# Start offsets of the narrow weight tiles in SBUF: one offset for both parts, or 64 pairs of eight line offsets

## The chip, the cores and the metric

The kernel runs on one core of a Trainium2 chip. The metric is the device time of one execution in microseconds. The kernel before takes 3164.23 us, the median of 3 runs (3163.09 to 3170.76).

## What is computed

Two transformer-like blocks stand one behind the other, on 256 tokens (and, in the first block, 256 context tokens) of width 1024, all in fp32. The first block has two layers: half an FFN, a mixer, half an FFN; the mixer of layer 0 is a Fourier transform, that of layer 1 a bidirectional retention. The second block has two layers of FFN, mixer (HGRN2 scan and dilated window attention) and FFN. From the reference, cut:

```python
def swiglu(h, w_gate, w_up, w_down):
    return (jax.nn.silu(h @ w_gate) * (h @ w_up)) @ w_down

def half_ffn(t, m, j):
    h = modulate(rmsnorm(t, norm_g[l, j]), m[3 * j], m[3 * j + 1])
    return t + 0.5 * m[3 * j + 2] * swiglu(h, ...)

def retention_layer(h_lat, h_ctx, w_in, w_out, decay, cos, sin, need_ctx_out):
    qc, kc, vc, gc = ret_project(h_ctx, w_in)
    ...
    ql, kl, vl, gl = ret_project(h_lat, w_in)
    ...
    y_lat = ret_output(yl, gl, w_out)

for l in range(DEPTH):                                   # the second block
    x = x + 0.5 * swiglu_2(rmsnorm_2(x, ffn1_norm[l]), ffn1_w_in[l], ffn1_w_out[l])
    h = rmsnorm_2(x, mix_norm[l])
    hq, hf, hi, hg, aq, ak, av, ga, gb = jnp.split(h @ w_in[l], split_idx, axis=-1)
    ...
    x = x + merged @ w_out[l]
    x = x + 0.5 * swiglu_2(rmsnorm_2(x, ffn2_norm[l]), ffn2_w_in[l], ffn2_w_out[l])
```

Nearly all arithmetic is in the products of activations with weights, which are most of the 506 MB that the kernel reads from HBM.

## The kernel before

**Three matmuls for a product.** Every fp32 operand is split into an upper part, rounded to the format float32r, and a lower part, the rest. A product is three float32r matmuls, `mm3` (L270): upper by upper (L272), upper by lower (L273) and lower by upper (L274), summed in PSUM. A matmul has a stationary operand of 128 x 128, which a weight load (PEld) brings into the array, and a moving operand of 256, 258 or 512 columns. Each of the three has a weight load of its own.

**Weights.** `get` (L205) and `getw` (L222) hand out weight tiles in an order that a first, empty pass over the program has recorded (`plan`). `_dma` (L151) loads 1 MiB into a tile `raw`; `_split` (L159) makes the upper part `wh` from it on ScalarE (ACT, L166) and the lower part `wl` on VectorE (DVE, L167). There are three buffers each of `wh` and `wl`. Each has 2048 + 128 elements of 4 bytes per partition, 8704 bytes, and begins at a multiple of 512 bytes. The data begin `at` bytes into the buffer, for `wh` and `wl` alike: 0 for WIDE tiles, whose moving operand has 512 columns, 64 for NARROW ones, with 256 columns, 192 for MOVING ones. L164 and L165:

```python
wh = self.wsp.tile([128, 2048 + PAD // 4], F32R, name="wh", tag="wh")[:, at // 4:]
wl = self.wsp.tile([128, 2048 + PAD // 4], F32R, name="wl", tag="wl")[:, at // 4:]
```

**The two uses of a tile.** `gemm_t` (L566) has the weights stationary and the activations moving: three matmuls for each of 8 slices k of 128 rows, then the same for the next 128 output columns. In the trace their names read `mm<-s,wh` and `mm<-s,wl`. `gemm_n` (L594) has the activations stationary and 256 columns of weights moving (`mm<-wh,s`, `mm<-wl,s`). Activations lie in tiles `s`, slots of 2048 bytes that begin at multiples of 512 bytes. So in `gemm_t` the moving operand begins at a multiple of 512, and the stationary one `at` bytes behind one; in `gemm_n` it is the other way round. Products of two activations (`mm<-s,s`) have both at multiples of 512.

**The order of the work.** It is written out by hand: `body` (L1728) calls the layers one after the other, and `tick` puts a piece of other work (norms, the scan, attention) between two groups of matmuls. From `M.retention` (L1787) on the stream has 256 columns, apart from eight 512-column matmul groups of the keys in the retention layer (WIDE), and apart from the FFN behind the retention layer (`M.ffn(..., shift=True)`, L1795): there the tokens carry two more columns, 258 in all, and the tiles' offsets come from the table SHIFTED, 22 numbers from 12 to 208, most of them no multiple of 64. Retention's values and the mixers' `unit_n` (L1249) use `gemm_n`.

Of the kernel before, what the change touches and what calls it, by code (L numbers as in the profile page):

```python
# [10 lines left out]
F32R = mybir.dt.float32r  # L11
# [8 lines left out]
KT = 8  # L20
# [9 lines left out]
SCRATCH = 1024  # L30
GAP = 2048 - SCRATCH - 128

WIDE, NARROW, MOVING, PAD = 0, 64, 192, 512
SHIFTED = (12, 68, 72, 76, 80, 84, 52, 44, 204, 200, 208, 196, 140, 136, 132, 144, 40, 36, 100, 88, 160, 176)

VEC = [("c", 8), ("c_ctx", 8), ("ada_b", 144), ("norm_g", 48), ("final_g", 8), ("four_b", 8),
       ("ffn1_norm_2", 16), ("mix_norm_2", 16), ("ffn2_norm_2", 16), ("hgrn_lb_logits_2", 16),
# [53 lines left out]
class Ker:  # L91
    def __init__(self, tc, I, out, plan):
        self.tc, self.nc, self.I, self.out = tc, tc.nc, I, out
        self.V, self.A, self.T = self.nc.vector, self.nc.scalar, self.nc.tensor
        self.free = deque(range(NSLOT))
        self.where = {}
        self.plan = plan
        self.asked = []
        self.nraw = NRAW
        self.ndma = self.nspl = self.nget = 0  # L100
        self.wget, self.wsplit, self.hold = -1, 0, None
        self.rawt, self.splt = {}, {}
        self.bg = deque()
        self.urgent = deque()
        self.pend = deque()
        self.subs = deque()
        self.late = {}
        self.chains = []
        self.turn = 0
        self.uid = 0  # L110
        self.quiet = False
        self.lazy = False
        self.splim = None

    def pools(self, ctx):
# [43 lines left out]
    def _split(self, i):  # L159
        src, raw, at = self.plan[i]  # L160
        if raw:
            return
        t, v, n = self.rawt.pop(i)
        wh = self.wsp.tile([128, 2048 + PAD // 4], F32R, name="wh", tag="wh")[:, at // 4:]  # L164
        wl = self.wsp.tile([128, 2048 + PAD // 4], F32R, name="wl", tag="wl")[:, at // 4:]  # L165
        self.A.activation(wh[:, :n], t[:, :n], AF.Copy)  # L166
        self.subs.append((i, lambda: self.V.tensor_sub(wl[:, :n], t[:, :n], wh[:, :n].bitcast(F32))))  # L167
        k = src.shape[1]
        self.splt[i] = (wh[:, :n].rearrange("p (k c) -> p k c", k=k),
                        wl[:, :n].rearrange("p (k c) -> p k c", k=k))  # L170
# [48 lines left out]
            return self.rawt.pop(i)[1]  # L219
        return self.splt.pop(i)  # L220

    def getw(self, w, k0, k1, c0, c1, at=NARROW):  # L222
        return self.get(w.rearrange("(k p) m -> p k m", p=128)[:, k0:k1, c0:c1], at=at)


# [133 lines left out]
class Model(Ker):  # L359
# [345 lines left out]
    def ffn(self, X, wg, wu, wd, resid, after=None, shift=False):  # L705
        n = N2 + 2 if shift else N2
        cx, c = slice(0, n), slice(0, N2)
        for hi, (f0, f1) in enumerate(self.HALVES):
            G = Split(self, f1 - f0, N2)
            for f in range(f0, f1, 2):  # L710
                at = (SHIFTED[f], SHIFTED[f + 1]) if shift else (NARROW, NARROW)
                ug = self.getw(wg, 0, KT, 128 * f, 128 * f + 256, at[0])
                pg = [self.mm([128, n]) for _ in range(2)]
                for m in self.pair_t(pg, ug, X, cx, f == 0):
                    self.tick()
                uu = self.getw(wu, 0, KT, 128 * f, 128 * f + 256, at[1])
                pu = [self.mm([128, n]) for _ in range(2)]
                for m in range(2):
                    self.gemm_t(pu[m], uu, X, m, cx, 0, KT, True, True)
                    if f:  # L720
                        self.ffn_act(G, f - f0 + m, pg[m], pu[m], N2, self.rb, shift)
                    self.tick()
                if f == 0:
                    self.drain_urgent()
                    for m in range(2):
                        self.ffn_act(G, m, pg[m], pu[m], N2, self.rb, shift)
            if hi == 1:
                X.rel()
            self.flush()
            km = (f0 + f1) // 2  # L730
            for mp in range(4):
                pd = [self.mm([128, N2]) for _ in range(2)]
                if hi == 1 and mp == 3:
                    self.splim = self.nget + 3
                for k0, k1 in ((f0, km), (km, f1)):
                    u = self.getw(wd, k0, k1, 256 * mp, 256 * mp + 256)
                    for m in range(2):
                        self.gemm_t(pd[m], u, G, m, c, k0, k1, k0 == f0, k1 == f1, f0)
                        if k1 == f1:
                            resid(2 * mp + m, pd[m])  # L740
                            if after and hi == 1:
                                after(2 * mp + m)
                            self.tick()
            self.resume()
            G.rel()
# [502 lines left out]

    def unit_n(self, X, n, off):  # L1249
        c = self.COLS[n] + off  # L1250
        u = self.getw(self.w_in, 0, KT, c, c + 256, MOVING)
        ps = self.mm([128, 2, 256])
        for tt in range(2):
            self.gemm_n(ps[:, tt], u, X, tt)
            self.tick()
        return ps
# [471 lines left out]
def body(M, stop):  # L1728
    I, out = M.I, M.out
    upto = STOPS.index(stop or "all")  # L1730

    def dump():
        M.nc.sync.dma_start(out.rearrange("(k p) t -> p k t", p=128), M.x[:, :, :out.shape[1]])

    def w(l, j):
        return I["ffn_w_gate"][l, j], I["ffn_w_up"][l, j], I["ffn_w_down"][l, j]

    M.consts()
    first, r, xr = [], [], []

    def sums(s):
        for d in range(KT):
            M.stat(d, STREAM[s])

    H = Split(M, KT, N1)
    M.splim = LATE - 1
    sums(0)

    def latent():
        xr.append(M.lead(0, r[0]))  # L1750
        sums(1)
    M.ada_first(0, {2: lambda: r.append(M.rstd(LAT)), 4: latent})
    M.ada_first(1, {0: lambda: r.append(M.rstd(CTX)), 4: lambda: xr.append(M.lead(1, r[1]))})
    M.splim = LATE
    M.lazy = True
    first.append(M.getw(I["ffn_w_gate"][0, 0], 0, KT, 0, 256))
    M.lazy = False
    M.rel(M.sc32)
    M.lead_end(xr[0], 0, H, 0, KT)
    M.splim = LATE + 1  # L1760
    M.catch_up()
    M.urgent.extend([lambda d=d: M.lead_end(xr[1], 1, H, d, d + 4) for d in range(0, KT, 4)])
    M.bg.append(M.ada_silu)
    half = [lambda d, s, j=j: M.cm[:, 8 * j + d, s:s + 1] for j in range(2)]
    for ch in range(2, 8):
        M.bg.extend(M.ada_steps(0, ch))
    H = M.ffn2s(H, *w(0, 0), half[0], 1, M.dft_load, (5, 8, 1), first[0])
    if upto == 0:
        return dump()
    H = M.fourier(H, 2)  # L1770
    if upto == 1:
        return dump()
    for l, ch in ((0, 8), (1, 0), (1, 1), (1, 2), (1, 3)):
        M.bg.extend(M.ada_steps(l, ch))
    H = M.ffn2s(H, *w(0, 1), half[1], 0)
    if upto == 2:
        return dump()
    for ch in range(4, 9):
        M.bg.extend(M.ada_steps(1, ch))
    H = M.ffn2s(H, *w(1, 0), half[0], 1, M.ret_prep, (2, 1, 4))  # L1780
    while M.bg:
        M.tick()
    M.rel(*M.cb[0], *M.cb[1])
    if upto == 3:
        return dump()

    M.retention(H, lambda: M.shifted_begin(2), M.pre)  # L1787
    X = M.pre_end()
    if upto == 4:
        return dump()  # L1790
    M.final_begin()

    def resid(d, ps):
        M.resid(d, ps, half[1], LAT)
    M.ffn(X, *w(1, 1), resid, M.final_pre, shift=True)  # L1795
    if upto == 5:
        return dump()
    X = M.final_end()
    if upto == 6:
        M.drain_urgent()  # L1800
        M.tick()
        return dump()
    ov = out.rearrange("(k p) t -> p k t", p=128)
    for l in range(2):
        M.pre_begin("mix_norm_2", l)

        def ww(j):
            wi = I[f"ffn{j}_w_in_2"][l]
            return wi[:, :FF], wi[:, FF:], I[f"ffn{j}_w_out_2"][l]
        M.ffn(X, *ww(1), M.resid_half, M.pre)  # L1810
        if upto == 7 + 2 * l:
            return dump()
        X = M.mixer(l, M.pre_end())
        if upto == 8 + 2 * l:
            return dump()
        if l == 0:
            M.pre_begin("ffn1_norm_2", 1)
            M.ffn(X, *ww(2), M.resid_half, M.pre)
            X = M.pre_end()
        else:  # L1820
            M.ffn(X, *ww(2), M.resid_half, lambda d: M.nc.sync.dma_start(ov[:, d], M.x[:, d, :N2]))
# [28 lines left out]
```

## Time and profile before

| | |
|---|---|
| median of 3 runs | 3164.23 us (3163.09 to 3170.76) |
| the profiled execution | 3162.56 us |
| its span, first to last instruction | 3160.8 us |
| granted TensorE clock, mean | 0.996 of 2.4 GHz |
| TensorE busy (PE) | 3121.8 us, 99% |
| weight loads (PEld) | 2928.3 us, 93% |
| VectorE (DVE) | 2192.4 us, 69% |
| ScalarE (ACT) | 1368.3 us, 43% |
| DMA | 510.69 MB, 162 GB/s |

Matmuls are pipelined: a record lasts some 280 ns, but the next one begins 113 to 120 ns after it. What a matmul costs is the step from one start to the next. It is read from a stretch without idle time as its length over the number of matmuls in it, less 2.4 that had begun before the stretch (280 ns over a step). The retention layer begins at 1214.9 us of the span, the FFN with 258 columns at 1508.4, the second block at 1712.

### The profile page before, as it was taken

What the parts mean: (1) busy time and instruction counts of PE and PEld (TensorE: products, weight loads), DVE (VectorE), ACT (ScalarE), POOL (GpSimd) and SP (SyncE); (2) the same over time, 40 slices, a digit from 0 to 9 for tenths busy, and PEclk for the clock granted to TensorE, in tenths of its full rate; (3) what the DMA queues carried; (4) which work ended last, traced back from release to release, by engine and by line L of the source; (5) the groups of instructions that cost most, each with busy time, mean ns of one, the idle gap of its engine ahead of it and who ended that gap; (6) DMA issues with size and microseconds to landing.
All of it is one profiled execution on the core that took longest, in us unless ns stands there. A gap on an engine that the chain in (4) does not pass through costs nothing.

```text
span 3160.8 us, 53819 instructions
## 1 busy us (share of the span) xinstructions
PE 3121.8 (99%) x22520; PEld 2928.3 (93%) x22520; DVE 2192.4 (69%) x4077; ACT 1368.3 (43%) x1945; POOL 0.5 (0%) x5
## 2 busy tenths in 40 slices
PE   7999999999999999999999999999999999999999
PEld 5888898888888889999999999999999999999999
DVE  6797578874666537566767678867756668877755
ACT  3223353222422225443545456654545446655543
POOL 0000000000000000000000000000000000000000
PEclk9999999999999999999999999999999999999999
DMA  7465414563246533233555654444555655444563
GB/s 285 166 224 178 136 54 134 182 204 123 91 156 216 185 107 108 94 123 119 170 189 188 201 188 152 160 147 134 186 190 185 198 184 171 152 156 134 177 198 121
DMA packets 431699, 510.69 MB, mean 162 GB/s; under 512 B 8800, under 2 KB 396128, under 8 KB 431456
## 3 DMA queue, kind: packets, MB, share of 16 engines
q1 hardware_dynamic: 428736, 503.35, 48.0%
q10 hardware_dynamic: 2720, 3.90, 0.4%
q8 instruction: 177, 2.90, 0.4%
q14 instruction: 66, 0.54, 0.0%
HBM read 506.16 MB, written 1.05 MB: 160 GB/s over the span
## 4 chain that ended last, share of the span: by engine, by line
PE 92%; DVE 5%; ACT 1%; issue 1%; DMA 1%; SPq 0%; ACTq 0%; DVEq 0%
PE mm L272 29%; PE mm L274 29%; PE mm L273 29%; PE mm L1465 2%; DVE wl L167 1%; ACT wh L166 1%; DVE x L672 1%; PE mm L1624 1%; DVE s L523 0%; DMA raw<-in_ada_n 0%; PE aux L1674 0%; PE mm L1608 0%; DVE s L520 0%; DVE sqs L483 0%; PE mm L580 0%
## 5 line engine op out<-in xcount | busy, mean ns | idle before, releaser
L272 PE MATMUL mm<-s,wh 128*128 128x256 f32 (+2 forms) x5872 | 1813.5, 309 | 3.5 <-ACT s L521 2.5
L273 PE MATMUL mm<-s,wh 128*128 128x256 f32 (+2 forms) x5872 | 1804.7, 307 | 2.9 <-DVE s L523 0.8
L274 PE MATMUL mm<-s,wl 128*128 128x256 f32 (+2 forms) x5872 | 1803.3, 307 | 3.2 <-DVE wl L167 3.1
L273 PEld LDWEIGHTS mm<-s,wh 128*128 128x128 f32 x5872 | 1112.6, 189 | 63.0 <-DVE s L523 4.1
L274 PEld LDWEIGHTS mm<-s,wl 128*128 128x128 f32 x5872 | 1108.6, 189 | 61.5 <-DVE wl L167 4.8
L272 PEld LDWEIGHTS mm<-s,wh 128*128 128x128 f32 x5872 | 1107.6, 189 | 62.4 <-ACT s L521 3.7
L167 DVE TENSOR_TENSOR wl<-raw,wh 128x2048 fp32r<-128x2048 f32 (+2 forms) x438 | 928.9, 2123 | 239.2 <-ACT wh L166 239.1
L166 ACT ACTIVATE wh<-raw 128x2048 fp32r<-128x2048 f32 (+2 forms) x438 | 777.1, 1779 | 594.6 <-PE mm L273 221.3
L457 DVE SCALAR_TENSOR_TENSOR jk<-raw,s 128x512 bf16<-128x512 f32 x448 | 309.2, 690 | 12.2
L272 PE MATMUL mm<-wh,s 128*128 128x256 f32 x960 | 273.6, 285 | 0.0
L767 ACT ACTIVATE s<-tmp 128x256 fp32r<-128x256 f32 (+1 forms) x176 | 87.8, 499 | 418.4 <-DVE tmp L753 320.3
L273 PE MATMUL mm<-wl,s 128*128 128x256 f32 x960 | 267.4, 279 | 0.0
L274 PE MATMUL mm<-wh,s 128*128 128x256 f32 x960 | 267.3, 278 | 0.0
L753 DVE TENSOR_TENSOR tmp<-tmp,mm 128x512 f32<-128x512 f32 x66 | 45.3, 686 | 196.7 <-PE mm L274 161.2
L273 PEld LDWEIGHTS mm<-wl,s 128*128 128x128 f32 x960 | 180.9, 188 | 0.2
L272 PEld LDWEIGHTS mm<-wh,s 128*128 128x128 f32 x960 | 180.8, 188 | 0.3
L274 PEld LDWEIGHTS mm<-wh,s 128*128 128x128 f32 x960 | 180.5, 188 | 0.0
L672 DVE SCALAR_TENSOR_TENSOR x<-mm,cm,x 128x256 f32<-128x256 f32 x160 | 71.8, 479 | 106.6 <-PE mm L274 106.5
L769 DVE TENSOR_TENSOR s<-tmp,s 128x256 fp32r<-128x256 f32 (+1 forms) x176 | 91.3, 519 | 2.2 <-ACT s L767 0.5
L765 DVE TENSOR_TENSOR tmp<-mm,sqs 128x256 f32<-128x256 f32 x88 | 36.8, 419 | 67.9 <-PE mm L274 67.7
L764 ACT ACTIVATE tmp<-tmp 128x256 f32<-128x256 f32 x88 | 36.2, 412 | 103.8 <-DVE tmp L763 103.7
L772 DVE SCALAR_TENSOR_TENSOR x<-mm,x 128x256 f32<-128x256 f32 x64 | 27.0, 423 | 53.9 <-PE mm L274 53.7
(247 smaller groups left out, 2028.5 us busy)
## 6 DMA issues: line engine op xcount, KB each, us to landing
raw<-in_ffn_w_in SPq DMA_DIRECT2D x88, 1024.0 KB, 4.9
raw<-in_w_in SPq DMA_DIRECT2D x84, 1024.0 KB, 4.8
raw<-in_ada_t SPq DMA_DIRECT2D x64, 1024.0 KB, 5.2
raw<-in_ffn_w_gate SPq DMA_DIRECT2D x44, 1024.0 KB, 5.1
raw<-in_ffn_w_up SPq DMA_DIRECT2D x44, 1024.0 KB, 5.1
raw<-in_ret_w_in SPq DMA_DIRECT2D x24, 1024.0 KB, 4.9
raw<-in_ffn_w_out SPq DMA_DIRECT2D x32, 768.0 KB, 4.6
raw<-in_ffn_w_down SPq DMA_DIRECT2D x32, 640.0 KB, 4.0
```

The lines of the kernel that those rows point to most:

```text
L166: self.A.activation(wh[:, :n], t[:, :n], AF.Copy)
L167: self.subs.append((i, lambda: self.V.tensor_sub(wl[:, :n], t[:, :n], wh[:, :n].bitcast(F32))))
L272: T.matmul(ps, ah, bh, start=first, stop=False)
L273: T.matmul(ps, ah, bl, start=False, stop=False)
L274: T.matmul(ps, al, bh, start=False, stop=last)
L457: V.scalar_tensor_tensor(jk, r[:, j, 512 * i:512 * i + 512], 1.0, self.cb[s][i], OP.mult, OP.mult, accum_out=a[:, 2 * q + j, s, i:i + 1])
L672: self.V.scalar_tensor_tensor(self.x[:, d, e], ps[:, e.start - c.start:e.stop - c.start], gate(d, s), self.x[:, d, e], OP.mult, OP.add)
L753: V.tensor_mul(g, sg, pu)
L765: V.tensor_mul(g, pu, rb)
L767: A.activation(G.h(f), g, AF.Copy)
L769: self.defer(lambda: V.tensor_sub(G.l(f), g, G.h(f).bitcast(F32)))
L1465: T.matmul(ps[:m, a, b], kc, qc, start=True, stop=True)
```

## The change

`getw` without an offset numbers the tiles. Up to the retention layer both parts still begin at 64. From there on (`M.later = True`) tile number 8i + j has its upper part at 64 j bytes and its lower part at 64 ((3j + i) mod 8) bytes; over 64 tiles these are all 64 pairs of 0, 64, ..., 448. The table SHIFTED and the offset MOVING go: the FFN with 258 columns and `unit_n` take pairs too. WIDE tiles stay at 0. The instructions of every engine are the same ones in the same order; start addresses alone differ, in 12,930 matmuls, in their weight loads, and in the ACT and DVE instructions that write `wh` and `wl`.

```diff
-WIDE, NARROW, MOVING, PAD = 0, 64, 192, 512
-SHIFTED = (12, 68, 72, 76, 80, 84, 52, 44, 204, 200, 208, 196, 140, 136, 132, 144, 40, 36, 100, 88, 160, 176)
+WIDE, NARROW, PAD = (0, 0), (64, 64), 512
...
+        self.later, self.narrow = False, 0
...
-        wh = self.wsp.tile([128, 2048 + PAD // 4], F32R, name="wh", tag="wh")[:, at // 4:]
-        wl = self.wsp.tile([128, 2048 + PAD // 4], F32R, name="wl", tag="wl")[:, at // 4:]
+        wh = self.wsp.tile([128, 2048 + PAD // 4], F32R, name="wh", tag="wh")[:, at[0] // 4:]
+        wl = self.wsp.tile([128, 2048 + PAD // 4], F32R, name="wl", tag="wl")[:, at[1] // 4:]
...
-    def getw(self, w, k0, k1, c0, c1, at=NARROW):
+    def getw(self, w, k0, k1, c0, c1, at=None):
+        if at is None:
+            i, j = divmod(self.narrow, 8)
+            at = (64 * j, 64 * ((3 * j + i) % 8)) if self.later else NARROW
+            self.narrow += 1
         return self.get(w.rearrange("(k p) m -> p k m", p=128)[:, k0:k1, c0:c1], at=at)
...
             for f in range(f0, f1, 2):
-                at = (SHIFTED[f], SHIFTED[f + 1]) if shift else (NARROW, NARROW)
-                ug = self.getw(wg, 0, KT, 128 * f, 128 * f + 256, at[0])
+                ug = self.getw(wg, 0, KT, 128 * f, 128 * f + 256)
...
-        u = self.getw(self.w_in, 0, KT, c, c + 256, MOVING)
+        u = self.getw(self.w_in, 0, KT, c, c + 256)
...
+    M.later = True
     M.retention(H, lambda: M.shifted_begin(2), M.pre)
```

## Rows read from the trace of the kernel before

**Rows 1.** The page: span, and part 1, busy time of each engine.
```profile
span 3160.8 us, 53819 instructions
...
PE 3121.8 (99%) x22520; PEld 2928.3 (93%) x22520; DVE 2192.4 (69%) x4077; ACT 1368.3 (43%) x1945; POOL 0.5 (0%) x5
```

**Rows 2.** The page, part 4: the chain that ended last, by engine.
```profile
PE 92%; DVE 5%; ACT 1%; issue 1%; DMA 1%; SPq 0%; ACTq 0%; DVEq 0%
```

**Rows 3.** Who waited for whom, PE alone: total us, times, longest us.
```profile
PE mm L274 <- DVE wl L167: 3.1, 5, 0.9
```

**Rows 4.** Windows, PE alone: start:end, length, busy us (matmuls in it), clock, DMA share, GB/s.
```profile
1275.00:1280.00 5.00, 5.00 (x44) 1.00 0.41 143
1508.40:1579.30 70.90, 70.03 (x584) 1.00 0.51 162
1613.30:1671.00 57.70, 57.70 (x483) 1.00 0.49 152
1717.00:1887.00 170.00, 170.00 (x1503) 1.00 0.61 196
...
2440.00:2612.00 172.00, 172.00 (x1520) 1.00 0.59 192
2990.00:3157.00 167.00, 167.00 (x1420) 1.00 0.50 163
```

**Rows 5.** Timeline of PE from 400.37, every third instruction: start us, length us, instruction.
```profile
400.37 0.28 PE L272 MATMUL mm<-s,wh 128*128 128x256 f32 x1
...
400.71 0.28 PE L272 MATMUL mm<-s,s 128*128 128x256 f32 x1
...
401.07 0.28 PE L272 MATMUL mm<-s,s 128*128 128x256 f32 x1
...
401.43 0.28 PE L272 MATMUL mm<-s,s 128*128 128x256 f32 x1
```

**Rows 6.** Timeline of PE from 2071.67, every third instruction.
```profile
2071.67 0.28 PE L272 MATMUL mm<-wh,s 128*128 128x256 f32 x1
...
2072.01 0.28 PE L272 MATMUL mm<-wh,s 128*128 128x256 f32 x1
...
2072.35 0.28 PE L272 MATMUL mm<-s,wh 128*128 128x256 f32 x1
...
2072.70 0.28 PE L272 MATMUL mm<-s,wh 128*128 128x256 f32 x1
...
2073.05 0.28 PE L272 MATMUL mm<-s,wh 128*128 128x256 f32 x1
```

**Rows 7.** Timeline of PE from 1899.78, every third instruction.
```profile
1899.78 0.28 PE L272 MATMUL mm<-s,wh 128*128 128x256 f32 x1
...
1900.13 0.29 PE L272 MATMUL mm<-wh,s 128*128 128x256 f32 x1
...
1900.49 0.28 PE L272 MATMUL mm<-wh,s 128*128 128x256 f32 x1
...
1900.83 0.28 PE L272 MATMUL mm<-wh,s 128*128 128x256 f32 x1
```

**Rows 8.** Groups of PE by form from 1214.9 on: count, busy us, mean ns, idle before.
```profile
L273 PE MATMUL mm<-s,wh 128*128 128x256 f32 x3569 | 997.1, 279 | 1.9 <-DVE s L1352 0.7 <-DVE s L1108 0.3 <-DVE s L523 0.3
L273 PE MATMUL mm<-wl,s 128*128 128x256 f32 x960 | 267.4, 279 | 0.0
L273 PE MATMUL mm<-s,wh 128*128 128x258 f32 x352 | 99.5, 283 | 0.0
```

**Rows 9.** The same of 1717:1887, then of 2990:3157.
```profile
L273 PE MATMUL mm<-s,wh 128*128 128x256 f32 x501 | 138.3, 276 | 0.0
...
L273 PE MATMUL mm<-s,wh 128*128 128x256 f32 x474 | 133.2, 281 | 0.0
```

**Rows 10.** Groups of DVE, the lower part's split: of 1613.3:1671, then of 2990:3157.
```profile
L167 DVE TENSOR_TENSOR wl<-raw,wh 128x2048 fp32r<-128x2048 f32 (+1 forms) x11 | 23.6, 2143 | 8.1 <-ACT wh L166 8.1
...
L167 DVE TENSOR_TENSOR wl<-raw,wh 128x2048 fp32r<-128x2048 f32 (+2 forms) x34 | 67.1, 1975 | 27.5 <-ACT wh L166 27.5
```

More of the change, by code (lines that the diff above doesn't have):

```diff
@@ L715, in ffn @@
                     self.tick()
-                uu = self.getw(wu, 0, KT, 128 * f, 128 * f + 256, at[1])
+                uu = self.getw(wu, 0, KT, 128 * f, 128 * f + 256)
                 pu = [self.mm([128, n]) for _ in range(2)]
```

## The prediction

> **What bounds the kernel now.** I read the page's busy times first: PE 99%, weight loads 93%, VectorE 69%, ScalarE 43% [rows 1]. The chain that ended last is PE for 92% [rows 2], and of PE's waits for a part of a weight tile there are five, 3.1 us in all [rows 3]. So the time is the number of matmuls times the step from one to the next. The edit takes away no matmul and moves none. It can act only on the step, or on the splits that write the tiles.
>
> Then I read the step, stretch by stretch, from the windows. It isn't one number, though shape and granted clock (1.00, the 2.4 GHz level) are the same [rows 4]:
> - **short**, 113.3 ns: the first FFN of the second block, 1717 to 1887 us. 170 us / (1503 - 2.4). Its twin in the next layer has 172 / (1520 - 2.4) = 113.3.
> - **middle**, 117.8 ns: the last FFN, 2990 to 3157. 167 / (1420 - 2.4).
> - **long**, 120.2 ns: products of two activations in the retention layer, 1275 to 1280. 5.00 / (44 - 2.4). The FFN with 258 columns has 70.03 / (584 - 2.4) = 120.4 in its first half and 57.7 / (483 - 2.4) = 120.1 in its second.
>
> Short and middle occur for the same tiles at the same offset, 64 bytes for both parts, hundreds of matmuls on end. So the offset alone doesn't fix the step; how the stream came into the stretch does too. What an offset does at a border without a wait, three timelines tell; three steps are 0.34 us if short, 0.35 if middle, 0.36 if long.
> - Up to 400.71 the stream is short, with weights at 64 and activations at 0. Then products of two activations begin, both at 0, and every three steps take 0.36 [rows 5]. The short step is lost at once.
> - Up to 2072.35 it is short with the moving weights at 192 and the stationary activations at 0; with stationary weights at 64 it is middle, 0.35 [rows 6]. Lost again.
> - At 1900.13 the reverse: from stationary weights at 64 to moving ones at 192, 0.35, then 0.36, then 0.34 [rows 7]. Here a change of offset wins the short step.
>
> So: the short step stays only while nothing changes, and another offset may set the stream into another step.
>
> **The change, part by part.** From 1214.9 us on, line L273 has 3569 matmuls with stationary and 960 with moving weights of 256 columns; times three lines, 10,707 and 2,880, together 13,587. With 258 columns there are 352 x 3 = 1,056 [rows 8]. How many are short now I take from the mean length of a record, which follows the step: 276 ns in the short stretch, 281 in the middle one [rows 9]. Both forms have 279 over the whole part [rows 8]. (281 - 279) / (281 - 276) = 40% short, 5,435; 60% middle, 8,152.
>
> 1. *Offsets differ from tile to tile.* A tile lasts 30 to 48 matmuls, and now each one brings another pair, where two FFNs ran through some 1,500 matmuls with one offset. Two of the three borders above lose the short step, and the one that wins it lies between the other two uses of a tile. I take it that the 5,435 become middle: 5,435 x (117.8 - 113.3) = +24.5 us. Bounds: all 8,152 middle ones become short, -36.7 us; or everything becomes long, 5,435 x 6.9 + 8,152 x 2.4 = +57.1 us. I choose the middle step because it is nearest to most rows: it is what the same operands fall into when they don't keep the short one.
> 2. *Both parts differ within a tile.* The three matmuls of a slice load upper, upper and lower part, so in 56 of 64 pairs the offset changes twice in three matmuls. No row shows that. If each change only costs what the border at 1900.13 cost, 0.02 us, the price is unbounded by the trace short of the long step in 1. I count nothing beside it.
> 3. *Line 0 is among the eight.* Offset 0 against activations at 0 is the pair of operands that has the long step. 8 of 64 pairs have their upper part there (two of three loads), 8 their lower part (one of three): (16 + 8) / 192 = 1/8 of the loads. 13,587 / 8 x (120.2 - 117.8) = +4.1 us. Bounds 0 and, if 256 acts as 0 does, +8.2. That it may is read from 64 against 0 and 0 against 192: differences of 64 and -192, equal but for 256, and both know the short step.
> 4. *Some short steps remain or are won*, as at 1900.13. An eighth of term 1: -3.1 us. Bounds are those of 1.
> 5. *The FFN with 258 columns* gives up a table of its own. It runs at 120.1 to 120.4 now, which is the long step already. Nothing, between -6.2 (1,056 x 5.9, all as short as the short step with two columns more, 114.2) and +1.
> 6. *The splits.* Where the table's offsets apply, the lower part takes 2143 ns, else 1975 [rows 10]: 0.17 us less for each of 22 tiles. It lies beside the matmuls, whose waits for it are 3.1 us in all, so nothing; a slower PE gives it more room still. Were that cover gone, it would be worth 3.7 us.
>
> Sum: 24.5 + 4.1 - 3.1 = **+25.5 us** on 3162.6, the profiled execution's own time (span 3160.8): 3188. The median of the runs shown is 1.7 above that execution, so I predict 3189 us.
>
> A rule speaks against all of it. The Trainium skill, "SBUF — State Buffer", section "Who interferes with whom", gives PE two independent read ports, one for the moving operand and one for weight loads, and says that "PE and ACT never wait on anyone". By that rule a start address would be worth nothing, and the time would stay at 3164. The trace disagrees here: with nothing but the start address of the stationary operand changed, the step goes from 113.3 to 120 ns at 400.71.
>
> **The rivals.**
> - *Long steps spread.* If multiples of 256 act as 0 does, 28 of 64 pairs hold at least one, and a tile may run long as a whole: 24.5 + 0.44 x 13,587 x 2.4 = +39 us, 3203. For it: the long step is what the 258 columns have at nearly all of their 22 offsets. Against: it is seen with 256 columns only where both operands begin at 0.
> - *Faster: the short step catches the stream.* A long run of the middle step can't leave it now, because nothing disturbs it; the FFN of 2990 to 3157 stays there to the end. Ever new offsets throw it out, as at 1900.13, and if the short step holds over all those pairs, the stream stays in it. With three quarters of the middle steps: -27.5 us, 3137. The point from which this decides is a share of short steps over today's 40%. Against: two of three borders lost the short step, and one of them by going to offset 0, which the pairs hold.
> - *Nothing happens*, or losses and gains balance: 3164, within 0.3%, or 9.5 us, which is about what a measurement of this kernel tells from no change. For it: stretches of both kinds exist now, and a new mix may come out at 40% again.
> - That the change doesn't do what it says I leave at under one in a hundred: the flag is set in the pass that records the plan and in the one that uses it.
>
> **How the numbers follow.** The forecast, 3180 to 3198, has 0.48; long steps spread 0.22; the short step catches 0.16; nothing 0.14. Faster by over 0.3% 0.16, within it 0.14, slower 0.70. The range goes from 3150, which leaves out most of the faster case, to 3214, nearly the bound with everything long (3221).
>
> **What would show it.** In the profile after, the stretch of the second block's first FFN holds some 1,440 matmuls in 170 us instead of 1,503; the mean record of L273 with 256 columns goes from 279 to 281 ns; the mean of the 258 columns stays at 283. Waits of PE for `wl` stay at some 3 us. I am wrong if the FFN at 1717 keeps 113 ns, or if the last FFN falls from 117.8 to it; and wrong in size if windows there show 120 or more.

## The result: 3185.0 us, and the profile after

| | before | after |
|---|---|---|
| median of 3 runs, us | 3164.23 (3163.09 to 3170.76) | 3185.04 (3184.93 to 3185.19) |
| profiled execution, us | 3162.6 | 3185.0 |
| its span, us | 3160.8 | 3183.2 |

The ratio is 1.006, with an interval of 1.0037 to 1.0083: slower. The forecast was 3189, its case 3180 to 3198.

The page of the changed kernel: the span, the busy time of each engine, and the chain that ended last by engine.

```profile
span 3183.2 us, 53819 instructions
...
PE 3144.2 (99%) x22520; PEld 2950.9 (93%) x22520; DVE 2193.2 (69%) x4077; ACT 1367.7 (43%) x1945; POOL 0.5 (0%) x5
...
PE 93%; DVE 5%; ACT 1%; issue 1%; DMA 1%; SPq 0%; ACTq 0%; DVEq 0%
```

Against [rows 1, 2], the counts of instructions are the same on every engine, VectorE and ScalarE are as busy as they were, and PE's busy time alone has grown by 22.4 us, as the span has. PE's waits for the lower part of a weight tile are these:

```profile
PE mm L279 <- DVE wl L168: 2.4, 5, 1.1
```

That is 2.4 us where [rows 3] have 3.1. So nothing new is waited for; the matmuls stand further apart. The windows of PE alone show where (start:end, length, busy us, matmuls in it, clock, DMA share, GB/s):

```profile
1508.40:1579.30 70.90, 70.51 (x583) 1.00 0.51 162
1613.30:1671.00 57.70, 57.70 (x481) 1.00 0.49 154
1717.00:1887.00 170.00, 170.00 (x1450) 1.00 0.58 189
2440.00:2612.00 172.00, 172.00 (x1466) 1.00 0.55 178
...
3010.00:3177.00 167.00, 167.00 (x1422) 1.00 0.50 164
```

The first FFN of the second block held 1503 matmuls in 170 us [rows 4] and holds 1450: the step went from 113.3 to 170 / (1450 - 2.4) = 117.4 ns. Its twin went from 113.3 to 117.5. The last FFN, moved 20 us later, keeps 167 / (1422 - 2.4) = 117.6, where it had 117.8. The granted clock is 1.00 throughout. The mean records by form, from the retention layer on, agree:

```profile
L277 PE MATMUL mm<-s,wh 128*128 128x256 f32 x3569 | 1009.4, 283 | 1.9 <-ACT s L1355 1.1 <-ACT s L526 0.8
L278 PE MATMUL mm<-s,wh 128*128 128x256 f32 x3569 | 1001.7, 281 | 1.8 <-DVE s L1356 0.7 <-DVE s L1112 0.3 <-DVE s L528 0.2
...
L278 PE MATMUL mm<-wl,s 128*128 128x256 f32 x960 | 270.1, 281 | 0.0
...
L278 PE MATMUL mm<-s,wh 128*128 128x258 f32 x352 | 99.7, 283 | 0.0
```

L278 is L273 of before: 279 became 281 with stationary and with moving weights, 258 columns stay at 283 [rows 8].

**Where the 22.4 us are.** From the start times of all matmuls of both traces I took the step from each weight matmul to the next, from the retention layer on, without the steps over 131 ns, in which PE waited or did something else. Stationary weights with 256 columns: 115.86 ns before, 117.54 after, times some 10,540: +17.7 us. Moving weights: 116.06 and 118.41, times 2,806: +6.6. With 258 columns: 120.12 and 120.88, times 1,052: +0.8. That is 25.1; the longer steps gave back 2.7. Steps under 115 ns were 43% of the stationary ones and 39% of the moving ones before; after, 20% and 7%.

**Which tiles are slow.** The same start times, tile by tile, gave the mean step for each pair of offsets. In the 8 x 8 table the twelve classes with a 0 or a 128 in them repeat after four offsets, 256 bytes, within 0.4 ns. In the four classes of 64 and 192 alone the tiles of one pair differ by up to 5 ns: these are the pairs that can have the short step or a longer one, and whether they repeat too is left to a run of its own below. Modulo 256, for stationary weights (ns; down: upper part, across: lower part):

```
upper\lower     0      64     128     192
   0         119.75  117.88  119.10  117.84
  64         117.88  114.75  118.22  114.27
 128         118.29  117.98  118.62  116.77
 192         117.74  117.64  117.75  115.96
```

A piece of the timeline shows it. These are the first matmuls of five tiles in a row of 36 matmuls each, at (448, 0), (0, 256), (64, 448), (128, 128) and (192, 320); start us, length us, instruction:

```profile
1783.61 0.28 PE L277 MATMUL mm<-s,wh 128*128 128x256 f32 x1
...
1787.85 0.28 PE L277 MATMUL mm<-s,wh 128*128 128x256 f32 x1
...
1792.17 0.28 PE L277 MATMUL mm<-s,wh 128*128 128x256 f32 x1
...
1796.27 0.28 PE L277 MATMUL mm<-s,wh 128*128 128x256 f32 x1
...
1800.53 0.28 PE L277 MATMUL mm<-s,wh 128*128 128x256 f32 x1
```

36 matmuls take 4.24 us at (448, 0), 117.8 ns each; 4.32 at (0, 256), 120.0; 4.10 at (64, 448), 113.9; 4.26 at (128, 128), 118.3. So the tile at (64, 448) is in the short step between neighbours that are not. All 14 tiles of that class, 64 with 192, end in the short step (113.3 to 114.3 ns over their last twelve steps); all 14 with both parts at 0 modulo 256 end at 120.

### The profile page after: what moved, and what is told of

The parts are those of the page before. It is cut to its first block, busy times and chain, and to the rows that moved or that the text cites. A ratio compares the mean times of both kernels' runs of the same rounds, so it can differ in the third digit from the quotient of the medians.

```text
span 3183.2 us, 53819 instructions
## 1 busy us (share of the span) xinstructions
PE 3144.2 (99%) x22520; PEld 2950.9 (93%) x22520; DVE 2193.2 (69%) x4077; ACT 1367.7 (43%) x1945; POOL 0.5 (0%) x5
## 4 chain that ended last, share of the span: by engine, by line
PE 93%; DVE 5%; ACT 1%; issue 1%; DMA 1%; SPq 0%; ACTq 0%; DVEq 0%
PE mm L277 29%; PE mm L279 29%; PE mm L278 29%; PE mm L1469 2%; DVE wl L168 1%; DVE x L677 1%; PE mm L1628 1%; DVE s L528 0%; ACT wh L167 0%; PE aux L1678 0%; DMA raw<-in_ada_n 0%; PE mm L1612 0%; DVE s L525 0%; DVE sqs L488 0%; PE mm L585 0%
## 5 line engine op out<-in xcount | busy, mean ns | idle before, releaser
L278 PE MATMUL mm<-s,wh 128*128 128x256 f32 (+2 forms) x5872 | 1808.7, 308 | 2.7 <-DVE s L1356 0.7
L278 PEld LDWEIGHTS mm<-s,wh 128*128 128x128 f32 x5872 | 1108.0, 189 | 62.8 <-DVE s L528 4.1
L278 PE MATMUL mm<-wl,s 128*128 128x256 f32 x960 | 270.1, 281 | 0.0
L278 PEld LDWEIGHTS mm<-wl,s 128*128 128x128 f32 x960 | 181.2, 189 | 0.2
```

The source lines that it names most:

```text
L278: T.matmul(ps, ah, bl, start=False, stop=False)
```

## Experiments

Diffs are against the changed kernel, unless said otherwise. The kernel before ran beside each group on the same chip: a median of 3162.25 us with e1, e2, e3 and e5 (3155.91 to 3164.43), 3157.06 with e4, e6, e7 and e8 (3156.47 to 3161.97), 3162.53 with e9, e10 and e11 (3156.44 to 3169.48). It has two groups of run times of its own, below and above 3160, and the medians differ by which of them prevailed: ratios of different groups of experiments can differ by 0.2% for that alone. Whether a kernel is faster than the kernel before goes by the ratio; kernels of different groups are compared by their own times and steps.

My first theory was that each pair of offsets has a step of its own, whatever came before. Its rival was the prediction's: what costs is that the offset changes.

**One pair for all stationary tiles, and the same pair swapped.** Moving tiles and the 258-column FFN have the offsets that they have in the kernel before. The edit of the first, cut; the second has (192, 64):

```diff
-            at = (64 * j, 64 * ((3 * j + i) % 8)) if self.later else NARROW
+            at = (64, 192)
...
```

There is no `later` in it, nor in the edits below that show none: they also reach 1,344 matmuls ahead of the retention layer, whose tiles name no offset of their own.

> The kernel before, with one edit: the lower part of a NARROW tile begins at 192, the upper stays at 64; moving weights and the 258-column FFN as before. Theory (the step is set by the two lines modulo 256 bytes and by how the stream came in; upper at 64 with lower at 192 pulls every stream into the short step): all 14 tiles of that pair in the trace after the change ended at 113.3 ns, whatever came before. So nearly all of the 10,700 matmuls with stationary weights run at 113.3 to 114: 10,700 x (115.9 - 113.6) = 25 us off, 3139 us (3132 to 3146). Rival (which step a stretch has is luck of entry, the pair is not it): short and middle mixed as before, 3164 within 10 us.

> The same as the run with 64 and 192, the two offsets swapped: upper part at 192, lower at 64. Theory: the order matters, since two of three weight loads take the upper part. In the trace after the change 11 of 15 tiles of this pair ended at 118.6 to 119.4 ns, 4 stayed short. So 10,700 x (118.5 - 115.9) = 28 us more, 3192 us (3175 to 3200). Rival (what counts is that the two parts lie two lines apart): as the run with 64 and 192, 3139. Second rival (luck of entry): 3164 within 10.

With (64, 192): 3139.62 us, ratio 0.9938 (0.9923 to 0.9953), as the theory had it. The stationary steps from the retention layer on fall from 115.86 to 113.73 ns, 22.4 us; the tiles ahead of it, which the theory left out, let that layer begin 3.4 us earlier. With (192, 64): 3177.03, ratio 1.0061 (1.0041 to 1.0081). The two kernels differ in nothing but which part has which offset, and lie 37 us apart by their medians. The second is 15 us better than expected, and its runs scatter from 3165.69 to 3181.41, which a step that the pair alone sets doesn't do. PE's windows, of (64, 192):

```profile
1717.00:1887.00 170.00, 170.00 (x1502) 1.00 0.60 195
2440.00:2612.00 172.00, 172.00 (x1519) 1.00 0.60 192
2990.00:3157.00 167.00, 144.53 (x1276) 1.00 0.45 145
```

and of (192, 64):

```profile
1717.00:1887.00 170.00, 170.00 (x1502) 1.00 0.59 190
2440.00:2612.00 172.00, 172.00 (x1449) 1.00 0.56 182
```

In the first all three FFNs are short, the last one too (it is over 22 us before the window ends; 144.53 / (1276 - 2.4) = 113.5). In the second one FFN is short throughout and its twin at 172 / (1449 - 2.4) = 118.9 throughout, in the same execution, with the same pair. So what the stream brings in counts as well, and the theory was not whole.

**All offsets 256 bytes further** than in the kernel before: stationary tiles at 320, moving ones at 448.

```diff
-            at = (64 * j, 64 * ((3 * j + i) % 8)) if self.later else NARROW
+            at = (320, 320)
...
```

> The kernel before with 256 bytes added to its offsets: NARROW 320 for 64 (both parts), moving weights 448 for 192 and, in the retention layer, 320 for 64; the 258-column FFN as before. Theory (only the line modulo 256 bytes counts): the same steps in the same stretches, 3164 us within 3. Rival (all eight lines differ): the mix of steps changes, by as much as 10,700 x 2 ns = 20 us either way.

3156.94 us, ratio 0.9995 (0.9985 to 1.0005): the same. Its ten runs lie in two groups, 3156 to 3158 and 3163 to 3164, as those of the kernel before do. The profiled execution, of 3155.8, shows what may tell them apart:

```profile
2990.00:3157.00 167.00, 160.88 (x1420) 1.00 0.51 164
```

The last FFN does in 160.88 us what takes 167 in [rows 4]: it is short here (160.88 / (1420 - 2.4) = 113.5) and was middle there. That FFN alone makes 6.1 of the 6.8 us between this execution and the profiled one of before (3162.6). One execution of either group was profiled, so that the groups differ by this FFN alone is likely and not shown.

**Moving tiles at equal offsets.** The change as it is, but moving tiles have both parts at 192 again (64 for `v_unit`); the numbering goes on as if they had been counted.

```diff
+            at = fix or ((64 * j, 64 * ((3 * j + i) % 8)) if self.later else NARROW)
...
```

> The changed kernel, but tiles whose weights move keep equal offsets as before (192 in the mixers, 64 in retention); the numbering of all others stays. Theory (a moving operand that begins on another line from one matmul to the next can never keep the short step; with equal offsets it can): the 2,800 matmuls with moving weights go from 118.3 ns back to about 116: 6.4 us off the changed kernel's 3185, 3179 us (3176 to 3181). Rival (moving tiles cost nothing of their own): 3185 within 2.

3179.07 us, ratio 1.0062 (1.0047 to 1.0077), 6.0 below the changed kernel. The moving steps go from 118.41 back to 116.11 ns, so the +6.6 us of the moving tiles and their place are confirmed. That unequal parts are the cause is not: the edit also takes the offsets 0 and 128 away from these tiles. Their lines, by form:

```profile
L278 PE MATMUL mm<-wl,s 128*128 128x256 f32 x960 | 267.4, 279 | 0.0
L279 PE MATMUL mm<-wh,s 128*128 128x256 f32 x960 | 267.4, 279 | 0.0
```

**Equal parts, offset 0 alone, odd offsets alone.** Three edits of the same line, one for each:

```diff
-            at = (64 * j, 64 * ((3 * j + i) % 8)) if self.later else NARROW
+            at = (64 * j, 64 * j) if self.later else NARROW
+            at = (0, 0) if self.later else NARROW
+            at = (64 * (2 * (j % 4) + 1), 64 * (2 * ((3 * j + i) % 4) + 1)) if self.later else NARROW
```

> The change with both parts of each narrow tile at the same offset, 64 times (number modulo 8): the offset still moves from tile to tile, the parts of one tile no longer differ. Theory (each pair of offsets, taken modulo 256 bytes, has its own step, whatever came before): the trace of the changed kernel has steps of 119.75 ns for stationary tiles with both parts at offset 0 modulo 256, 115.0 at 64, 118.6 at 128, 116.0 at 192; their mean is 117.3 against 115.86 before, times 10,632 matmuls: +16 us; moving tiles by the same table 118.0 against 116.06, times 2,806: +5; 258 columns +1. That lies 3 us below the changed kernel: 3182 us (3177 to 3188). Rival (what costs is that the two parts of one tile differ): with equal parts the time goes back to 3164 (3159 to 3169).

> Every narrow tile from the retention layer on has both parts at offset 0, where before has 64 (moving ones 192): nothing changes from tile to tile or within a tile. Theory (offset 0 modulo 256 bytes is the long step by itself): 119.9 ns against 115.86 for 10,632 matmuls with stationary weights, +43 us, 119.8 against 116.06 for 2,806 with moving ones, +10; 258 columns stay at 120: 3217 us (3208 to 3224). Rival (an offset that stays the same lets the step settle at the short one as often as before, at any offset): 3164 (3155 to 3172).

> The change with only the four odd line offsets (64, 192, 320, 448), by their number in 16 pairs; offsets still move from tile to tile, and the two parts differ in 12 of 16 pairs. Theory (the pair of offsets decides): the four classes of the changed kernel's trace, 115.0 (64 with 64), 114.3 (64 with 192), 117.6 (192 with 64) and 116.0 ns (192 with 192), have a mean of 115.7 against 115.86 before: -1 us; moving tiles 117.2 against 116.06: +3; 258 columns +1: 3167 us (3155 to 3172, since 192 with 64 came out shorter where all tiles had it). Rival (what costs is that offsets change from tile to tile): as slow as the changed kernel, 3185 (3179 to 3190).

- Equal parts: **3190.18** us, ratio 1.0105 (1.0087 to 1.0123). Slower than the changed kernel: two offsets within a tile are not what costs. It is also 8 us more than the first theory said.
- Offset 0 alone: **3211.86**, ratio 1.0174 (1.0156 to 1.0192). Here nothing ever changes, and it is the slowest of all. Of 248 stationary tiles, 234 settle at 120.0 to 120.1.
- Odd offsets alone: **3147.74**, ratio 0.9969 (0.9957 to 0.998). Here the offsets change with every tile, and it is faster than before and 19 us below what the first theory said.

So the rival falls on both sides: a stream without changes can be the slowest, one that changes all the time fast. PE's window at the first FFN of the second block, with equal parts:

```profile
1717.00:1887.00 170.00, 170.00 (x1439) 1.00 0.57 186
```

with offset 0 alone:

```profile
1717.00:1887.00 170.00, 169.17 (x1411) 1.00 0.55 178
```

and with odd offsets alone:

```profile
1717.00:1887.00 170.00, 170.00 (x1502) 1.00 0.59 191
```

These are steps of 118.3, 120.1 and 113.4 ns. Both misses of the first theory have one pattern. Tiles at (64, 64) have 117.0 ns with equal parts, where nearly each comes behind a tile at 0, and 114.4 among odd offsets; (192, 64) has 117.6 in the changed kernel and 114.0 among odd offsets. So these pairs keep what they find. That made the second theory: **the step is handed on from tile to tile**; some pairs bring the short one, some break it, some keep it.

**Every eighth tile.** The kernel before, with every eighth of its (64, 64) tiles at another pair: (64, 192), (0, 0) or (128, 128). Everything else is as before. The edit of the first:

```diff
-            at = (64 * j, 64 * ((3 * j + i) % 8)) if self.later else NARROW
+            at = (64, 192) if j == 0 else (64, 64)
...
```

> The kernel before, with every eighth of the narrow tiles that lie at (64, 64) there at (64, 192). Theory (the short step is a state: a (64, 192) tile always brings it, and (64, 64) tiles keep it until something breaks it): the seven (64, 64) tiles behind each also run short, 114.4 ns as among the odd offsets in the run with odd offsets alone, and the stationary steps have a mean of 114.3 against 115.86: -17 us, 3147 us if the kernel before stands at 3164 (3140 to 3152, ratio 0.990 to 0.997). Rival (each pair has its own step and hands nothing on): an eighth of the tiles gains 2.1 ns, 10,632 / 8 x 2.1 = -3 us, 3161 us or a ratio of 0.999.

> The kernel before, with every eighth of its (64, 64) tiles at (0, 0). Theory (an offset of 0 modulo 256 bytes breaks the state, and (64, 64) finds it again late): the seven tiles behind have 117.0 ns, as (64, 64) had in the run with equal parts, the eighth 119.9; mean 117.4 against 115.86: +16 us, 3180 us (3174 to 3186, ratio 1.004 to 1.008). Rival (each pair has its own step): 10,632 / 8 x (119.9 - 115.86) = +5 us, 3169 us or a ratio of 1.002.

> The kernel before, with every eighth of its (64, 64) tiles at (128, 128). Theory (128 modulo 256 breaks the state as 0 does): 7/8 of the tiles at 117.0 and 1/8 at 118.7, mean 117.2 against 115.86: +14 us, 3178 us (3172 to 3184, ratio 1.003 to 1.007). Rival (only an offset of 0 breaks it; 128 costs in its own tiles alone): 10,632 / 8 x (118.7 - 115.86) = +4 us, 3168 us or a ratio of 1.001.

With (64, 192): 3148.57 us, ratio 0.9952 (0.9937 to 0.9967); the stationary mean is 114.6 ns, 114.3 expected. With (0, 0): 3177.34, ratio 1.0044 (1.0027 to 1.006); 117.2, 117.4 expected. Both go by the second theory: an eighth of the tiles moves the rest. With (128, 128): 3157.84, ratio 0.9984 (0.9975 to 0.9994); 115.4 ns. Neither side had that: these tiles cost nothing on the whole. That they help is not shown, since the kernel before takes 3156 to 3158 us itself in its lower group, and its like 256 bytes further has 115.2 ns there.

The first matmuls of tiles of 48 in a row show each case. With an eighth at (64, 192): a tile at (64, 64), the one at (64, 192) from 2445.34 on, then (64, 64) again.

```profile
2439.68 0.28 PE L278 MATMUL mm<-s,wh 128*128 128x256 f32 x1
...
2445.34 0.28 PE L278 MATMUL mm<-s,wh 128*128 128x256 f32 x1
...
2450.80 0.28 PE L278 MATMUL mm<-s,wh 128*128 128x256 f32 x1
...
2456.24 0.28 PE L278 MATMUL mm<-s,wh 128*128 128x256 f32 x1
```

5.66 us is 117.9 ns each; at (64, 192) 5.46, 113.8; the tile at (64, 64) behind it 5.44, 113.3. It had the middle step and now has the short one, at the same offsets. With an eighth at (0, 0), which begins at 1736.24:

```profile
1730.80 0.28 PE L278 MATMUL mm<-s,wh 128*128 128x256 f32 x1
...
1736.24 0.28 PE L278 MATMUL mm<-s,wh 128*128 128x256 f32 x1
...
1742.00 0.28 PE L278 MATMUL mm<-s,wh 128*128 128x256 f32 x1
...
1747.65 0.28 PE L278 MATMUL mm<-s,wh 128*128 128x256 f32 x1
```

113.3 ns, then 5.76 us or 120.0 at (0, 0), then 5.65 or 117.7 at (64, 64): the short step is gone, and this tile doesn't find it again. With an eighth at (128, 128), which begins at 1735.90:

```profile
1730.45 0.28 PE L278 MATMUL mm<-s,wh 128*128 128x256 f32 x1
...
1735.90 0.28 PE L278 MATMUL mm<-s,wh 128*128 128x256 f32 x1
...
1741.59 0.28 PE L278 MATMUL mm<-s,wh 128*128 128x256 f32 x1
...
1747.04 0.28 PE L278 MATMUL mm<-s,wh 128*128 128x256 f32 x1
```

113.5, then 5.69 us or 118.5 at (128, 128), then 5.45, 113.5 again.

The same over whole traces, stationary tiles that follow each other without a wait: in the kernel before, (64, 64) stays short in 85 of 95 cases and stays middle in 110 of 118. A (64, 192) tile behind a middle one turned short in 7 of 8. A (0, 0) tile went to the long step in 24 of 26 cases, and of the 26 tiles at (64, 64) behind a long one, 1 was short. Behind a (128, 128) tile, 20 of 28 tiles at (64, 64) were short. The exceptions at (64, 64) in the kernel before have breaks in them: where at least twelve matmuls on either side of the border run on without a wait and without another matmul, the step was handed on each time, the short one in 74 of 74 cases, the middle one in 83 of 83. In the same kind of stretch (128, 128) does not simply hand on: of 16 short streams 12 were short behind it and 4 middle, and 3 of 3 middle ones turned short.

**One pair for everything.** Stationary tiles at (64, 192), those of the 258-column FFN too; moving tiles at (192, 192). No list, no numbering.

```diff
-            at = (64 * j, 64 * ((3 * j + i) % 8)) if self.later else NARROW
+            at = (64, 192)
...
-        u = self.getw(self.w_in, 0, KT, c, c + 256)
+        u = self.getw(self.w_in, 0, KT, c, c + 256, (192, 192))
...
-                uv = self.getw(wi, 0, KT, c, c + 256)
+                uv = self.getw(wi, 0, KT, c, c + 256, (192, 192))
```

> One pair for all: every narrow stationary tile, those of the 258-column FFN too, has its upper part at 64 and its lower at 192, every moving tile both at 192; the list of offsets by FFN block and the numbering are gone. Theory: as the kernel with 64 and 192 (3139.6 us), less 8 moving tiles of 54 matmuls that go from 117.8 ns at offset 64 to 115.7 at 192, -1 us; the 258-column steps stay at 120 ns: 3138.7 us (3135 to 3142). Rival (the 258-column blocks need their spread offsets): their steps go to 122 ns as in the worst pairs of the changed kernel, 1,056 times 2 ns: 3141 (3140 to 3144).

3138.27 us (3137.82 to 3139.01), ratio 0.994 (0.9925 to 0.9956): faster than both kernels, by 47 us against the changed one, 3.5 of them ahead of the retention layer, where the changed kernel still has (64, 64). The eight moving tiles at 64 have 96 matmuls each, not 54; moving steps go from 116.06 to 115.68 ns, -1 us as expected. Of its stationary steps, 92% are short. The step with 258 columns has 120.39 ns against 120.12, so the list of offsets that it had is worth 0.3 us.

## Why the prediction was right, and where not

**The bound and the size hold.** PE is the bound, nothing waits anew, 3185 lies in the forecast's own case and 4 below its number. Of what was to be seen, 1,450 matmuls at 1717 instead of some 1,440, a mean record of 281, 258 columns at 283 and waits of 2.4 us all came. The three runs of the kernel before were all above 3163; 14 of its 35 later runs took 3156 to 3158.5, and against these the change costs 28 us, still near the forecast.

**The terms of the sum, measured.** Against the middle step of 117.8 ns, the weight matmuls with 256 columns stood 25.3 us lower in the trace before: so much there was to lose (term 1, 24.5). After the change, tiles with 64 and 192 alone still stand 5.9 us lower (term 4, 3.1); tiles with a 0 modulo 256 in them stand 3.4 higher (term 3, 4.1), and those with a 128 and no 0 1.5 higher, which had no term. 25.3 - 5.9 + 3.4 + 1.5 = 24.3, against 25.5 as predicted.

**Term 1** (short steps become middle, +24.5) had sign and size right and the reason wrong. "The short step stays only while nothing changes" falls with the odd offsets, which change with each tile and run at 114.2 ns on the mean, and with (0, 0), which never changes and runs at 119.9. What the border at 400.71 [rows 5] showed was not a change but an offset of 0 coming in; both operands begin there. Nor does "nothing but the start address" change at that border: the stationary operand itself is another, activations instead of weights. In the changed kernel short steps are lost because 188 of the 248 stationary tiles have a 0 or a 128 modulo 256 in them, and none of these settled under 116.7 ns; of the 60 with 64 and 192 alone, 36 ended short. By the prediction's reason the odd offsets alone would have cost as much; they gained. So the size came out partly by luck: the 64 pairs happen to be 48 with a 0 or a 128 in them.

**Term 2** (parts that differ within a tile, 0). For stationary tiles right on the whole: equal parts are slower still, and the best pair has two different offsets. For moving tiles it may be wrong: of those with unequal parts modulo 256, none settled short, 37 in the changed kernel and 24 with odd offsets alone. But equal parts at all eight offsets gave back only 1.4 us (117.90 ns against 118.41); the 6 us of the run with moving tiles at equal offsets needed 64 or 192 as well, and no run takes the two apart. In the sum term 1 covered it, because it treated the short steps of both kinds alike.

**Term 3** (+4.1, half-believing that 256 acts as 0). It does: the classes with a 0 in them repeat every 256 bytes, and the kernel with 256 added everywhere takes the same time. Its own price was about right, 3.4 us. What the term did not see is that a 0 also costs the tiles behind it: one tile in eight at (0, 0) cost 1.0044, or 14 us, of which its own steps make 5. In the changed kernel that loss lies within what term 1 counts.

**Term 4** (an eighth of the short steps remains, -3.1) was too low, by half: 20% of the stationary steps in the trace after are short, almost half of what there were, since (64, 192), a sixteenth of the pairs, brings the step and the other pairs of 64 and 192 can hold it.

**Term 5** (258 columns, 0): +0.8 us.

**Term 6** (the splits). No effect on the time, as said, but the row was misread. The groups of VectorE after, of 1613.3:1671 and then of 3010:3177:

```profile
L168 DVE TENSOR_TENSOR wl<-raw,wh 128x2048 fp32r<-128x2048 f32 (+1 forms) x11 | 23.6, 2142 | 8.1 <-ACT wh L167 8.1
...
L168 DVE TENSOR_TENSOR wl<-raw,wh 128x2048 fp32r<-128x2048 f32 (+2 forms) x34 | 67.1, 1975 | 26.3 <-ACT wh L167 26.3
```

The table is gone and the 2143 ns of [rows 10] stay, at 2142. So the difference between the two stretches was never the offsets'. The means mix tiles of different size: one of 2048 elements takes 2288 or 2289 ns in both stretches, before the change and after, and the second has more of the smaller ones (1536 and 1280).

**The rule.** The Trainium skill, "SBUF — State Buffer", section "Who interferes with whom", gives PE two independent read ports and says that PE never waits on anyone; the prediction took from it that a start address would be worth nothing. The runs do not bear that out: kernels that differ in start addresses alone take 3138.27 to 3211.86 us.

**The rivals.** *Nothing happens* is out. *Long steps spread* was right in its mechanism, multiples of 256, and is what the run with offset 0 alone shows; in the changed kernel only the stationary tiles with both parts there are long; the others with a 0 or a 128 have 116.8 to 119.1 ns. *The short step catches the stream* is real too: it happens with odd offsets or with (64, 192), and its point of decision is not the share of short steps but which pairs are among those that come up.

**Open.** Why a start offset sets the step at all, why the order of 64 and 192 matters, and why (128, 128) is mostly followed by the short step, no run here tells. Nor does one tell which breaks of the stream change the step that (64, 64) holds.

## What to carry to other kernels

Where PE is busy 99% of the time, the step from matmul to matmul is the thing to read, by windows, stretch by stretch: two stretches of the same tiles with different steps mean that something outside the instruction decides. Before spreading offsets over all values, run each candidate alone, and in a few tiles among others: a bad value can cost nearly three times what its own tiles lose (14 us against 5), and one good value in every tile was worth more here than any mix that was run. A kernel with two groups of run times may owe them to a stretch that is entered in one of two steps; a pair that always brings the same one seems to take the scatter away as well (3137.82 to 3139.01 in four runs, against 3156.47 to 3161.97 in the nine runs of the kernel before beside them).

## What was not expected of the hardware

- The step of a 256-column matmul with stationary weights, weight load and all, depends on where both parts of the weights begin, modulo 256 bytes: 113.3 ns at best, 120.0 at worst, most often 117.8 or 118.9 between them, with one shape and one granted clock.
- Which of two parts has which offset matters: the medians of (64, 192) and (192, 64) lie 37 us apart.
- The step outlives its cause: (64, 64) keeps the short step or the middle one for hundreds of matmuls, in the same kernel, and one FFN of some 1,400 matmuls can so differ by 6 us between two executions of kernels that are alike but for 256 bytes.
